# A decoder layer on one core: transposes of the probabilities and of half the gated sum taken from TensorE to VectorE and DMAs, and two FFN pairs computed by seven block products

## The chip, the core and the metric

The kernel runs on one core of one Trainium2 chip. The metric is the device time of one execution in microseconds (us). The engines are TensorE (PE; its weight loads PEld), VectorE (DVE), ScalarE (ACT), GpSimd (POOL) and SyncE (SP). Each takes its own queue of instructions in order, and semaphores let one engine wait for another. DMAs are issued from a queue of SP, ACT or POOL.

## What is computed

One layer of a hybrid decoder for 256 positions, width 1024, FFN width 2816, in float32:

```python
h = rmsnorm(x, norm1_g)
x_rnn, g_rnn, q, k, v, g_br = split(h @ w_in)
ya = rg_lru(causal_dwconv(x_rnn)) * gelu(g_rnn)
yb = attention(rmsnorm(q), rmsnorm(k), v)            # 8 heads of 128, causal
merged = sigmoid(g_A) * (ya @ w_proj_rnn) + sigmoid(g_B) * (yb @ w_proj_attn)
x = x + merged @ w_out
h = rmsnorm(x, norm2_g)
act = gelu(causal_dwconv(h @ w_up)) * (h @ w_gate)
x = x + act @ w_down
```

The sequence fits one block of the sparse attention, so attention is plain and causal. The 2816 FFN columns are 11 blocks of 256.

## The kernel before

**Numbers.** Every product of two float32 matrices is made of three matmuls: each operand is split into a high part (rounded to the format that PE takes) and a low part (the rest), and high·high, high·low and low·high are summed. `mm3` issues the three.

**Weights.** They come in chunks of 1 MB, 128 partitions by 2048. A chunk is loaded by SP into a buffer `raw`, ACT casts it into `hi` (three of them are cast by DVE, `DVE_HI`), DVE writes `lo` = raw - hi, and PE runs 24 matmuls of 128x512 on the two. There are 3 buffers for raw, 4 for hi and 3 for lo; a chunk's lo can be written only when the chunk that held the buffer has been used by PE. In the program before, chunks have numbers (`lo43`); in the one after they are named by their use (`loup0`).

**Stages.** First come the input projections (rx, rg, k, q, v, ga, gb), the recurrence and the attention, then pr and pa (the projections of the two branches), wo (the output projection) and the second norm, then the FFN. In the attention, `att_s` makes a head's scores and its softmax in `sm`, `att_t` transposes the probabilities with three PE transposes and splits them, and `att_o` multiplies them by v. `pa_evac` makes the gated sum `sgb`, and `m_t` transposes a quarter of it with four PE transposes into `mh` and `ml`, which wo reads: blocks 0 and 1 of wo read the first half, blocks 2 and 3 the second. The second norm transposes (`h2T`), multiplies by the norm's weight (`h200` is the first 128 positions, first half of the width; `h210` the second 128 positions) and splits into `h2h` and `h2l`.

**FFN.** Blocks are taken in five pairs and a last one. For pair p, `ffn_half` runs up and gate, each in two halves of the inner dimension (two chunks, 48 matmuls). ACT evacuates the sums into `fs`, and `turn` transposes them: DVE transposes 32x32 squares, four DMAs write to DRAM and one reads back, all issued by SP. Then come the convolution's taps (`fc`), gelu and the product with the gate, which is split into `fah` and `fal`, and `dn` (w_down, accumulated in `acc`) reads them. PE's order is: pair 0, pair 1, pair 2, dn0 dn1, pair 3, dn2 dn3, pair 4, the last block, dn4 to dn9, and the end.

**Order.** Nothing is scheduled by dependences. The program lists every operation and `Later.issue` hands them out in the order of the table `ORDER`, in which "+n" stands for n matmuls; every engine's queue is a part of that one sequence. All instructions therefore bear one line, 296 before and 180 after, and are told apart by their tiles.

Of the kernel before, what the change touches and what calls it, by code (L numbers as in the profile page):

```python
# [7 lines left out]
F32 = mybir.dt.float32  # L8
# [6 lines left out]
P = 128  # L15
# [14 lines left out]
HALVES, SMALLS, WARM, RAWS = 23, 10, 11, 3  # L30
AHEAD_S, AHEAD_L = 2, 3
DVE_HI = (39, 42, 43)
KEPT = {"upd": 2, "gtd": 2, "u": 1, "c": 2, "ah": 3, "al": 3, "s": 1}
UNITS = ("rx0 rx1 rx2 rx3 rg0 rg1 rg2 rg3 k0 k1 k2 k3 ri0 q0 q1 ri1 ga0 ga1 q2 q3 v0 v1 ga2 ga3 v2 v3 gb0 "
         "gb1 gb2 gb3 pr0 pr1 pr2 pr3 pa0 pa1 pa2 pa3")
AFTER = {
    "rx0.0": "s4 stats",
    "rg0.0": "ev0",
    "rg0.3": "ev1",
    "rg1.1": "rx0",  # L40
    "rg1.2": "s5 rx1",
    "rg1.3": "s6 ge0",
    "rg2.1": "xo0",
    "rg3.0": "rgr0",
    "rg3.1": "conv0",
    "rg3.2": "xo1",
    "rg3.3": "s7 ge1",
    "k0.0": "s8 s9",
    "k0.2": "rgr1 conv1",
    "k1.2": "s10 s11",  # L50
    "k1.3": "s12",
    "k2.2": "s13",
    "k2.3": "split0 decay",
    "k3.0": "gelu1 conv2 conv3 split1",
    "k3.3": "s14",
    "ri0.0": "s15",
    "ri0.2": "krs0 ks0",
    "q0.3": "krs1",
    "q1.2": "ks1",
    "q1.3": "s16 rk1",  # L60
    "ri1.3": "rk0",
    "ga0.1": "rq0",
    "ga1.1": "s17 Tk0",
    "q2.0": "s18",
    "q3.0": "s19",
    "q3.2": "Tq0",
    "v0.0": "s20",
    "v1.0": "Tk1",
    "v1.1": "qrs0",
    "v1.2": "S3 s21",  # L70
    "ga2.0": "S2",
    "ga2.1": "rq1 S1 Tq1",
    "ga2.2": "s22 S0 P3",
    "ga2.3": "s23",
    "ga3.0": "s24 s25 la0 la1",
    "ga3.1": "lb1",
    "ga3.2": "lc1 P1 lb0",
# [107 lines left out]
+1 435 +4 444 +1 445 +4 475 +8 446 +2 442 432 +3 391-392 +1 393 +1 464 +3 465 +2 476 +1 478 +8 472 +1 466 474 +1  # L185
# [114 lines left out]
def trunk_layer(ctx: ExitStack, tc: tile.TileContext, xT, x, vec, win_fm, win_tm, wri, wpr, wpa,  # L300
# [23 lines left out]
    class Act:  # L324
# [13 lines left out]
        def pair(self, c):  # L338
            return kt(self.half(c // 2))[:, 2 * (c % 2):2 * (c % 2) + 2, :]


    stream = []

    def add(src):
        stream.append(src)
        return len(stream) - 1

    def two(w, base, c):

        g, kh = c // 2, c % 2  # L350
# [839 lines left out]
```

## Time and profile before

| | before |
|---|---|
| time, median of 3 runs | 434.46 us (434.1 to 435.2) |
| span of the profiled execution; its page gives no other time of its own | 432.3 us |
| granted TensorE clock, mean | 1.000 |
| ACT table loads | 15, 1283 ns each |
| HBM read, written | 89.74 MB, 11.01 MB |
| DMAs of GpSimd's queue | none |

The page gives, for each engine, the time in which it was busy, then 40 slices of the span, and the chain of work that ended last, followed back from the last instruction. Groups of instructions are listed by tile as out<-in with the shape, the count, the busy time and the mean of one in ns, and the idle time ahead of them with what ended it. A timeline row begins with the start and the length in us. Matmuls overlap in PE, so the mean of one (389 ns for 128x512) is not the spacing of two.

### The profile page before, as it was taken

The numbers are of one execution on the slowest core, as the hardware profiler recorded it, in microseconds if no ns is written. First come the engines' busy times: TensorE is split into PE (matmuls) and PEld (weight loads), VectorE is DVE, ScalarE is ACT, GpSimd is POOL, SyncE is SP. The second block draws the span as 40 slices with busy tenths as digits, with TensorE's granted clock in tenths as the row PEclk, the third lists the DMA queues.
The fourth block names the chain that finished last, engine by engine and source line by source line (L and its number), as shares of the span: only waits on it lengthen the run. The fifth ranks groups of instructions, "written<-read, shape, count | busy, mean of one in ns | idle before, by whom it ended". The sixth has DMA issues, their size and how long they took to land.

```text
span 432.3 us, 5409 instructions
## 1 busy us (share of the span) xinstructions
PE 427.6 (99%) x1992; PEld 357.3 (83%) x1992; DVE 324.5 (75%) x417; ACT 271.2 (63%) x307; POOL 51.9 (12%) x101
## 2 busy tenths in 40 slices
PE   9999999999999999999999999999999999999996
PEld 8888888888887888888888888888888888888885
DVE  4867499899898999865666796587888667769633
ACT  5687596886999998853241364468566556456510
POOL 0022483567160000000000000000000000000000
PEclk9999999999999999999999999999999999999999
DMA  7997945999991844474453556898888688788402
GB/s 253 395 394 256 339 169 149 295 314 335 368 313 38 284 142 149 130 238 134 181 194 116 176 203 207 299 325 253 284 265 313 237 270 262 243 286 293 152 0 97
DMA packets 33833, 101.09 MB, mean 234 GB/s; under 512 B 3216, under 2 KB 14096, under 8 KB 30352
## 3 DMA queue, kind: packets, MB, share of 16 engines
q1 hardware_dynamic: 33664, 100.76, 69.1%
q8 instruction: 15, 0.25, 0.2%
q14 instruction: 10, 0.08, 0.0%
q10 hardware_dynamic: 144, 0.00, 0.0%
HBM read 89.74 MB, written 11.01 MB: 233 GB/s over the span
## 4 chain that ended last, share of the span: by engine, by line
PE 87%; DMA 5%; ACT 3%; DVE 2%; issue 2%; SPq 0%; ACTq 0%; DVEq 0%
PE acc L296 14%; PE up L296 13%; PE gt L296 13%; PE rx L296 5%; PE gb L296 5%; PE pr L296 5%; PE yo L296 5%; PE pa L296 5%; PE k L296 5%; PE rg L296 5%; DMA qm<-qd 3%; PE q L296 3%; PE last L296 3%; PE v L296 2%; DMA raw<-in_win_fm 2%
## 5 line engine op out<-in xcount | busy, mean ns | idle before, releaser
L296 DVE TENSOR_TENSOR lo<-raw,hi 128x2048 fp32r<-128x2048 f32 (+1 forms) x72 | 160.3, 2227 | 40.1 <-PE gt L296 10.5
L296 ACT CAST hi<-raw 128x2048 fp32r<-128x2048 f32 (+1 forms) x69 | 128.3, 1862 | 49.7 <-PE gt L296 11.8
L296 PE MATMUL up<-hi,h2h 128*128 128x512 f32 x80 | 31.3, 391 | 0.0
L296 PE MATMUL up<-hi,h2l 128*128 128x512 f32 x80 | 31.2, 389 | 0.0
L296 PE MATMUL up<-lo,h2h 128*128 128x512 f32 x80 | 31.1, 389 | 0.0
L296 PE MATMUL gt<-hi,h2h 128*128 128x512 f32 x80 | 31.1, 389 | 0.0
L296 PE MATMUL gt<-lo,h2h 128*128 128x512 f32 x80 | 31.1, 389 | 0.0
L296 PE MATMUL gt<-hi,h2l 128*128 128x512 f32 x80 | 31.1, 389 | 0.0
L296 PE MATMUL acc<-hi,fah 128*128 128x512 f32 x80 | 31.1, 389 | 0.0
L296 PE MATMUL acc<-lo,fah 128*128 128x512 f32 x80 | 31.1, 389 | 0.0
L296 PE MATMUL acc<-hi,fal 128*128 128x512 f32 x80 | 31.1, 389 | 0.0
L296 POOL TENSOR_TENSOR rsq<-rsq 128x8 f32<-128x8 f32 x32 | 19.2, 600 | 28.6 <-DVE rsq L296 26.3
L296 ACT ACT_TABLE_LOAD x15 | 19.2, 1283 | 1.4 <-PEq L1180 1.2
L296 DVE SCALAR_TENSOR_TENSOR fc<-fu,pv,fc 128x255 f32<-128x255 f32 (+1 forms) x40 | 17.3, 477 | 2.1 <-ACT fc L296 2.1
L296 ACT ACTIVATE fc<-fu,pv 128x256 f32<-128x256 f32 x20 | 10.8, 593 | 11.1 <-DVE fu L296 11.1
L296 PEld LDWEIGHTS up<-hi,h2l 128*128 128x128 f32 x80 | 15.0, 188 | 3.2
L296 PEld LDWEIGHTS acc<-lo,fah 128*128 128x128 f32 x80 | 15.0, 188 | 3.1
L296 PEld LDWEIGHTS acc<-hi,fal 128*128 128x128 f32 x80 | 15.0, 188 | 3.1
L296 PEld LDWEIGHTS gt<-hi,h2l 128*128 128x128 f32 x80 | 15.0, 188 | 3.1
L296 PEld LDWEIGHTS gt<-lo,h2h 128*128 128x128 f32 x80 | 15.0, 188 | 3.1
L296 PEld LDWEIGHTS gt<-hi,h2h 128*128 128x128 f32 x80 | 15.0, 188 | 3.1
L296 PEld LDWEIGHTS acc<-hi,fah 128*128 128x128 f32 x80 | 15.0, 188 | 3.1
(222 smaller groups left out, 1038.8 us busy)
## 6 DMA issues: line engine op xcount, KB each, us to landing
raw<-in_win_fm SPq DMA_DIRECT2D x12, 1024.0 KB, 7.6
raw<-in_win_tm SPq DMA_DIRECT2D x12, 1024.0 KB, 7.2
raw<-in_wdown SPq DMA_DIRECT2D x11, 1024.0 KB, 6.7
raw<-in_wup SPq DMA_DIRECT2D x10, 1024.0 KB, 5.3
raw<-in_wgate SPq DMA_DIRECT2D x10, 1024.0 KB, 7.3
raw<-in_wpr SPq DMA_DIRECT2D x4, 1024.0 KB, 4.8
raw<-in_wpa SPq DMA_DIRECT2D x4, 1024.0 KB, 4.9
raw<-in_wout SPq DMA_DIRECT2D x4, 1024.0 KB, 4.8
```

What stands on the lines that cost most here:

```text
L296: getattr(engine, name)(*map(real, a), **{n: real(v) for n, v in k.items()})
```

## The change

Five things change together, and the table of the order is written anew.

1. **Probabilities.** `att_t` uses `turn`, with 384 columns: a DVE transpose into `pd`, four DMAs to DRAM and one back into `sm`. The two parts of the split are read by `att_o` in the permuted order of columns, runs of 32.
2. **Gated sum.** Its first half is turned in the same way (`md`, `mm`), its second half by PE as before.
3. **FFN pairs 1 and 3.** For a pair, up and gate are one product of two 2x2 block matrices: positions (2 halves) by inner dimension (2 halves), times inner dimension by kind (up, gate). `group` computes it with seven block products in place of eight, from sums and differences of the blocks. `forms` makes four combinations of the normed activations once (R1, S2, S3, S4), and four weight sums are made for each pair: sums 1 and 3 by an accumulating DMA of GpSimd from DRAM into the raw buffer, sums 2 and 4 by DVE. Each product splits its operand (names `b00`, `t1`, `b10`, `b11`, `t2`, `t4`, `t3`) and runs 12 matmuls of 128x512.
4. **Copies.** The copies `fu` ahead of the taps go from DVE to ACT; no weight chunk's hi is cast by DVE any more.
5. **Buffers.** raw has 4 buffers (was 3), `fs` two, PSUM is one pool of eight banks, and the halves are 21 (were 23).

```diff
-HALVES, SMALLS, WARM, RAWS = 23, 10, 11, 3
-DVE_HI = (39, 42, 43)
-KEPT = {"upd": 2, "gtd": 2, "u": 1, "c": 2, "ah": 3, "al": 3, "s": 1}
+HALVES, SMALLS, WARM = 21, 10, 11
+BUFS = {"raw": 4, "hi": 4, "lo": 3}
+SUMS = "dvdv"
+KEPT = {"upd": 2, "gtd": 2, "u": 1, "c": 2, "ah": 3, "al": 3, "s": 2}
...
     def att_t(h):
-        sm = heads[h]
-        ps = bank(f"pt{h}")
-        for b in range(3):
-            nc.tensor.transpose(ps[:, b * P:(b + 1) * P], sm[:, b * P:(b + 1) * P], ident)
-        pth, ptl = small(f"pth{h}", 384, F32R), small(f"ptl{h}", 384, F32R)
-        split2(pth, ptl, ps[:, :3 * P])
+        turn(f"pm{h}", small(f"pd{h}", 384), probs[h], 3, probs[h])
+        a = small(f"ph{h}", 384, F32R), small(f"pl{h}", 384, F32R)
+        split2(*a, probs[h])
+        probs_t[h] = tuple(v.rearrange("p (i u a) -> p u i a", i=4, u=3) for v in a)
...
+        if MT[g]:
+            d = half(f"md{g}")
+            turn(f"mm{g}", d, sgb.half(g))
...
+            for t in range(2):
+                nc.scalar.copy(v(mh)[:, t], d[:, t])
+                nc.vector.tensor_sub(v(ml)[:, t], d[:, t], f(v(mh)[:, t]))
...
+    def forms(name, hi_, lo_, m, new):
...
+        r1, s3, s2, s4 = a11, a10, a00, a01
+        nc.vector.tensor_sub(r1, a11, a10)
+        nc.vector.tensor_sub(s3, a00, a10)
+        nc.vector.scalar_tensor_tensor(s2, r1, -1.0, a00, op0=OP.mult, op1=OP.subtract)
+        nc.vector.scalar_tensor_tensor(s4, a01, -1.0, s2, op0=OP.mult, op1=OP.subtract)
+        for n, v in (("R1", r1), ("S4", s4), ("S2", s2), ("S3", s3)):
+            h, l = new(f"{name}{n}h"), new(f"{name}{n}l")
+            split2(h, l, v)
...
+    def group(name, a, src, rs, nrs, out0, out1, cols=True):
...
+        x = load(f"{name}x", src[0][0])
+        y = load(f"{name}y", src[0][1]) if by["1"] + by["3"] != "dd" else None
+        w, z = load(f"{name}w", src[1][0]), load(f"{name}z", src[1][1])
...
+        product(ps["a"], a["a00"], part("b00", x), True)
+        nc.scalar.activation(o[1][0], ps["a"], AF.Copy, scale=r[0])
+        nc.scalar.activation(o[0][1], ps["a"], AF.Copy, scale=r[1])
+        add("1", x, y, src[0][1])
+        product(ps["c"], a["R1"], part("t1", x), True)
+        nc.scalar.activation(o[1][1], ps["c"], AF.Copy, scale=nrs[:, 1:2])
+        product(ps["a"], a["a01"], part("b10", w), False)
+        nc.scalar.activation(o[0][0], ps["a"], AF.Copy, scale=r[0])
+        product(ps["c"], a["S4"], part("b11", z), False)
+        add("2", x, z, src[1][1])
+        product(ps["b"], a["S2"], part("t2", x), True)
+        nc.vector.scalar_tensor_tensor(o[1][0], ps["b"], r[0], o[1][0], op0=OP.mult, op1=OP.add)
+        nc.vector.scalar_tensor_tensor(o[1][0], ps["c"], nrs[:, 0:1], o[1][0], op0=OP.mult, op1=OP.subtract)
+        add("4", w, x, None)
+        product(ps["d"], a["a11"], part("t4", w), True)
+            add("3", z, None, src[0][1])
+        product(ps["b"], a["S3"], part("t3", y), False)
+        nc.vector.scalar_tensor_tensor(o[0][1], ps["b"], r[1], o[0][1], op0=OP.mult, op1=OP.add)
+        nc.vector.tensor_sub(o[1][1], o[1][1], o[0][1])
+        nc.vector.scalar_tensor_tensor(o[0][1], ps["d"], r[1], o[0][1], op0=OP.mult, op1=OP.add)
...
-            nc.vector.tensor_copy(plain(u, t), d[:, t])
+            FU(plain(u, t), d[:, t])
```

In `add`, "v" is a `tensor_add` of DVE, and "d" a DMA of GpSimd with `accum_op` add, from DRAM. `FU` is ACT's copy. PE's order in the FFN is now: pair 0, the group of pair 1, pair 2, dn0 dn1, the group of pair 3, dn2 dn3, pair 4, and so on as before. `pr3` stands behind `pa1`, so that the second half of pa follows it directly.

**Places in the order.** DVE's queue at the second norm, before:

```order
L296 TENSOR_TENSOR h200_2220<-h2T00_2214,pv_215 128x512
L296 TENSOR_TENSOR h2l0_2233<-h200_2220,h2h0_2226 128x4x128
L296 TENSOR_TENSOR h210_2239<-h2T10_2229,pv_215 128x512
L296 TENSOR_TENSOR xs_181<-yo01_2123,xs_181 128x512
L296 TENSOR_TENSOR h2l0_2233<-h210_2239,h2h0_2226 128x4x128
L296 TENSOR_TENSOR lo43_2255<-raw43_2121,hi43_2195 128x2048
```

and after:

```order
L180 TENSOR_TENSOR h200_2254<-h2T00_2246,pv_133 128x512
L180 TENSOR_TENSOR h210_2272<-h2T10_2264,pv_133 128x512
L180 TENSOR_TENSOR h2l0_2277<-h200_2254,h2h0_2262 128x4x128
L180 TENSOR_TENSOR lof1b00_2283<-rawf1x_2094,hif1b00_2200 128x2048
L180 TENSOR_TENSOR h2l0_2277<-h210_2272,h2h0_2262 128x4x128
L180 TENSOR_TENSOR xs_118<-yo11_2161,xs_118 128x512
```

The long subtraction of a weight chunk, which stood behind the low part of h210, now stands ahead of it.

ACT's queue about the end of pair 0's gate, before (hi48 and hi49 are the two gate chunks of pair 1):

```order
L296 CAST hi48_2398<-raw48_2339 128x2048
L296 ACTIVATE fs0_2391<-up01_2261,rs2_2381 128x512
L296 ACTIVATE fs0_2391<-gt00_2315,rs2_2381 128x512
L296 ACTIVATE fs0_2391<-gt01_2320,rs2_2381 128x512
L296 CAST hi49_2443<-raw49_2373 128x2048
```

and after, where hif1b11 and hif1b10 belong to the group of pair 1:

```order
L180 CAST hif1b11_2445<-rawf1z_2318 128x2048
L180 ACTIVATE fs0_2438<-up01_2290,rs2_2377 128x512
L180 CAST hif1b10_2478<-rawf1w_2366 128x2048
L180 ACTIVATE fs0_2438<-gt00_2348,rs2_2377 128x512
L180 ACTIVATE fs0_2438<-gt01_2356,rs2_2377 128x512
```

A cast now stands ahead of the two evacuations of gate. DVE's queue over the same group, after:

```order
L180 TENSOR_TENSOR lof1t1_2442<-rawf1x_2094,hif1t1_2403 128x2048
L180 TENSOR_TENSOR rawf1x_2094<-rawf1x_2094,rawf1z_2318 128x2048
L180 STREAM_TRANSPOSE fupd0_2468<-fs0_2438 128x8x4x32
L180 TENSOR_TENSOR lof1b11_2476<-rawf1z_2318,hif1b11_2445 128x2048
L180 STREAM_TRANSPOSE fgtd0_2505<-fs0_2438 128x8x4x32
L180 TENSOR_TENSOR lof1b10_2512<-rawf1w_2366,hif1b10_2478 128x2048
L180 TENSOR_TENSOR rawf1w_2366<-rawf1w_2366,rawf1x_2094 128x2048
L180 TENSOR_TENSOR lof1t2_2542<-rawf1x_2094,hif1t2_2521 128x2048
L180 TENSOR_TENSOR lof1t4_2560<-rawf1w_2366,hif1t4_2546 128x2048
L180 TENSOR_TENSOR lof1t3_2582<-rawf1z_2318,hif1t3_2567 128x2048
```

Where four subtractions and two transposes stood for a pair, there are now seven subtractions and two sums about the two transposes, and the transpose of gate stands ahead of lof1b10.

DVE's queue from the middle of the group of pair 3 to dn2 and dn3, after:

```order
L180 TENSOR_TENSOR lof3b10_2900<-rawf3w_2768,hif3b10_2884 128x2048
L180 TENSOR_TENSOR rawf3w_2768<-rawf3w_2768,rawf3x_2601 128x2048
L180 TENSOR_TENSOR lof3t2_2929<-rawf3x_2601,hif3t2_2911 128x2048
L180 TENSOR_TENSOR lof3t4_2943<-rawf3w_2768,hif3t4_2931 128x2048
L180 SCALAR_TENSOR_TENSOR fc1_2863<-fu0_2579,pv_133,fc1_2863 128x255
L180 SCALAR_TENSOR_TENSOR fc1_2863<-fu0_2579,pv_133,fc1_2863 128x254 x4
L180 TENSOR_TENSOR lof3t3_2978<-rawf3z_2723,hif3t3_2951 128x2048
L180 SCALAR_TENSOR_TENSOR fs1_2503<-f3b_2956,rs2_2377,fs1_2503 128x512
L180 TENSOR_TENSOR fc1_2863<-fgtd1_2774,fc1_2863 128x4x128 x2
L180 TENSOR_TENSOR lodn2_3007<-rawdn2_2946,hidn2_2992 128x2048
L180 TENSOR_TENSOR fal1_3021<-fc1_2863,fah1_3010 128x1024
L180 TENSOR_TENSOR lodn3_3027<-rawdn3_2962,hidn3_3016 128x2048
```

All of these stand behind one another from the group's second product on. Before, fal1 stood ahead of the subtraction of pair 3's second chunk, with three more chunks behind it ahead of dn2.

More of the change, by code (lines that the diff above doesn't have):

```diff
@@ new lines @@
+TURN_ACT = ""
+KEPT = {"upd": 2, "gtd": 2, "u": 1, "c": 2, "ah": 3, "al": 3, "s": 2}
+PLAN = """
+rx rg0 rg1 rg2 rg3 decay k0 k1 k2 k3 ri0 q0 q1 ri1 ga0 ga1 q2 q3 v0 v1:3 S3 P3 v1 ga2:1 S2 P2 ga2:1 S1 P1 ga2:1 S0 P0 ga2 ga3 v2:2 S4 P4 v2
+v3:2 S5 P5 v3 O3 gb0:2 O2 gb0 gb1:1 S6 P6 gb1 gb2:1 S7 P7 gb2:1 O1 gb2 O0 gb3:2 O4 gb3 ya0 ya1 pr0 pr1:1 O5 pr1 pr2:2 O6
+pr2 pa0 O7 pa1 pr3 pa2 pa3 wo000 wo010 wo100 wo110 wo001 m2 wo011 wo101 m3 wo111 wo200 wo300 wo210 wo310 wo201 wo301
+n00 wo211 n10 wo311 up00:1 n01 up00:2 n11 up00 gt00 stats2 up01 gt01 G1 up20 up21 gt20 gt21 dn0 dn1 G3 dn2 dn3 up40 up41 gt40 gt41 last0 last1 dn4 dn5 dn6 dn7 dn8 dn9 end
@@ new lines, in trunk_layer, with load @@
+              "up": lambda c: two(wup, 0, c), "gt": lambda c: two(wgate, 0, c),
+              "last": lambda c: [w[NF - 1, :, c * 1024:(c + 1) * 1024] for w in (wup, wgate)],
+              "wo": lambda c: wout[c], "dn": lambda c: wdown[c]}
+    def load(name, src, pieces=1):
+        r = wp.tile([P, 2048], F32, tag="raw", name=f"raw{name}", bufs=BUFS["raw"])
+        if isinstance(src, list):
+            n = 2048 // len(src)
+            for a, v in enumerate(src):
+                nc.sync.dma_start(r[:, a * n:(a + 1) * n], v)
+        elif len(src.shape) == 3:
+            nc.sync.dma_start(r.rearrange("p (c n) -> p c n", c=2), src)
+        else:
+            n = src.shape[-1] // pieces
+            for a in range(pieces):
+                nc.sync.dma_start(r[:, a * n:(a + 1) * n], src[:, a * n:(a + 1) * n])
+        return r
@@ new lines, in split @@
+    def split(name, r, n=2048, on_dve=False, m=1):
+        h = wp.tile([P, 2048], F32R, tag="hi", name=f"hi{name}", bufs=BUFS["hi"])
+        l = wp.tile([P, 2048], F32R, tag="lo", name=f"lo{name}", bufs=BUFS["lo"])
+        if name in LO_DMA:
+            nc.scalar.copy(h[:, :n], r[:, :n])
+            nc.scalar.activation(l[:, :n], r[:, :n], AF.Copy, scale=-1.0)
+            nc.gpsimd.dma_start(l[:, :n], r[:, :n], accum_op=OP.add)
+            return h, l
+        for a in range(m):
+            s = slice(a * n // m, (a + 1) * n // m)
+            (nc.vector.tensor_copy if on_dve else nc.scalar.copy)(h[:, s], r[:, s])
+            nc.vector.tensor_sub(l[:, s], r[:, s], f(h[:, s]))
+        return h, l
@@ L419, in split2, with chunk @@
+    def chunk(kind, c, n=2048, **k):
+        return split(f"{kind}{c}", load(f"{kind}{c}", source[kind](c)), n, **k)
     def split2(dh, dl, src):
@@ L631, in rx_evac @@
         turned_x[g] = half(f"xd{g}")
-        turn(f"xm{g}", turned_x[g], scaled(half(f"xs{g}"), rx_ps[g], rs1), f"rx{g}")
+        turn(f"xm{g}", turned_x[g], scaled(half(f"xs{g}"), rx_ps[g], rs1))
     def rx_order(g):
@@ new lines, in rx_all @@
+    def rx_all():
+        for g in range(2):
+            rx_ps[g] = [bank(f"rx{g}{t}") for t in range(2)]
+        for a in range(KT // 2):
+            for g in range(2):
+                for cs in (slice(0, 1), slice(1, 2)) if (a, g) == (0, 0) else (slice(0, 2),):
+                    for kk in range(2):
+                        k = 2 * a + kk
+                        h, l = shi[a, g][:, cs, kk], slo[a, g][:, cs, kk]
+                        for n, (x, w) in enumerate(((xgh, h), (xgl, h), (xgh, l))):
+                            for t in range(2):
+                                nc.tensor.matmul(rx_ps[g][t].rearrange("p (c n) -> p c n", c=2)[:, cs],
+                                                 x[k][:, t * P:(t + 1) * P], w, start=k == n == cs.start == 0,
+                                                 stop=k == KT - 1 and n == 2, skip_group_check=True)
+        norm1_stats()
+        for g in range(2):
+            rx_evac(g)
+            rx_order(g)
+            for c in (2 * g, 2 * g + 1):
+                rx_conv(c)
+            ri_split(g)
@@ new lines, in unit @@
+    def unit(kind, c):
+        if kind == "ri":
+            w = chunk(kind, c, 1024)
+            for n4 in range(4):
+                ri(c, w, n4)
+                if n4 == 3:
+                    lru(c)
+                yield
+            return
+        w = chunk(kind, c)
+        g, kh = c // 2, c % 2
+        if not kh:
+            open_ps[kind] = [bank(f"{kind}{g}{t}") for t in range(2)]
+        ps = open_ps[kind]
+        for k4 in range(4):
+            tm_mm(ps, w, 4 * kh + k4, k4, *{"pr": (yah, yal), "pa": (ybh, ybl)}.get(kind, (xgh, xgl)),
+                  kind not in "qkv")
+            if kh and k4 == 3:
+                evac[kind](g, ps)
+            yield
@@ new lines, in x_forms, with rg_group @@
+    def x_forms():
+        m = {}
+        for t in range(2):
+            for kh in range(2):
+                v = m[t, kh] = small(f"xf{t}{kh}", 512)
+                nc.vector.tensor_mul(v.rearrange("p (k t) -> p k t", t=P), kt(xTs.half(kh))[:, :, t * P:(t + 1) * P],
+                                     g1[:, 4 * kh:4 * kh + 4, None].to_broadcast([P, 4, P]))
+        return forms("xf", xgh, xgl, m, lambda n: small(n, 512, F32R))
+    xf = []
+    def rg_group():
+        if not xf:
+            xf.extend((x_forms(), negative(rs1, "nrs1")))
+        s = [half(f"gs{g}") for g in range(2)]
+        src = [[source["rg"](2 * g + kh) for g in range(2)] for kh in range(2)]
+        yield from group("rg", xf[0], src, rs1, xf[1], *s)
+        for g in range(2):
+            rg_turn(g, s[g])
@@ L999, in norm2_stats @@
         rsqrt(ss2[:, 0, :], rs2, 1.0 / D, 2)
+        xf[:] = [forms("hf", h2h, h2l, h2, lambda n: small(n, 512, F32R)), negative(rs2, "nrs2")]
     acc, act, kept = {}, {}, {}
@@ L1018, in trunk_layer, with ffn_out, pair_act @@
     turned, gated = {}, {}
-    def pair_up(p):
+    FU = nc.scalar.copy
+    def ffn_out(kind, p, s):
+        d = half("fld") if kind == "last" else keep(kind + "d", p)
+        turn(f"{kind}m{p}", d, s)
+        v = d.rearrange("p (i t c b) -> p t c i b", i=4, t=2, c=4)
+        turned["last" if kind == "last" else (kind, p)] = v
+        if kind == "last":
+            last_block()
+        elif ("up", p) in turned and ("gt", p) in turned:
+            pair_act(p)
+    def pair_act(p):
         d = turned["up", p]
@@ L1125, in trunk_layer @@
+    NP = NF // 2
+    for token in PLAN.split():
+        step(token)
     with tc.manual_schedule():
```

606 lines of the change are left out of this document (199 added, 407 removed), and 82 rows, old and new, of the table ORDER.

## The prediction

> **What bounds the kernel now.** I read the page's busy shares and its slices first, then the chain that ended last, then what TensorE (PE) waited for, to see whether any other engine is ever late.
>
> ```profile
> span 432.3 us, 5409 instructions
> PE 427.6 (99%) x1992; PEld 357.3 (83%) x1992; DVE 324.5 (75%) x417; ACT 271.2 (63%) x307; POOL 51.9 (12%) x101
> PE   9999999999999999999999999999999999999996
> DVE  4867499899898999865666796587888667769633
> PEclk9999999999999999999999999999999999999999
> PE 87%; DMA 5%; ACT 3%; DVE 2%; issue 2%; SPq 0%; ACTq 0%; DVEq 0%
> PE warm L296 <- DVE ones L296: 1.0, 1, 1.0
> PE pt L296 <- DVE sm L296: 0.4, 1, 0.4
> 271.19 10.88 PE up L296 x48
> 282.07 10.88 PE gt L296 x48
> ```
>
> PE is busy in every slice but the last, and inside the program it waits once, 0.4 us. The two last rows are steps of the chain (start, length): 48 matmuls of 128x512 in 10.88 us, so **226.7 ns each, back to back**. The span is the sum of PE's work, so a matmul taken away is worth its whole time, and any lateness that the change brings to DVE, ACT or a DMA costs its whole time too. I use this spacing, not the mean of one instruction, which counts overlap twice. The span is 432.3 us and the median of the runs 434.46: 2.16 us lie outside the span, and I add them at the end.
>
> **What leaves PE.**
>
> ```profile
> 139.16 0.70 PE pt L296 x3
> 148.09 0.70 PE s L296 x6
> 151.52 0.33 PE pt L296 x3
> 141.93 0.64 PE o L296 x6
> 225.67 0.44 PE mT L296 x4
> ```
>
> Pairs 1 and 3 of the FFN had 96 matmuls each and have seven products of 12, 84: 24 fewer, 24 x 0.2267 = 5.44 us. The probabilities' transposes were 8 groups of 3 at 0.33, 2.64 us, and the first took 0.70, which holds PE's only wait: 0.37 more. Of four mT groups two go to the stream transpose: 2 x 0.44 = 0.88. Together **9.33 us**. Against it, the o matmuls now read the probabilities in runs of 32 elements. The s group, whose operands are already read in such runs, takes 0.70 where o takes 0.64: 0.06 x 8 = 0.5 us, with ends 0 and 0.5. PE's own work falls by **8.8 us**.
>
> **What DVE and ACT get.** The rows with their means, and a stretch of DVE's timeline for the spacing:
>
> ```profile
> L296 DVE TENSOR_TENSOR lo<-raw,hi 128x2048 fp32r<-128x2048 f32 (+1 forms) x72 | 160.3, 2227 | 40.1 <-PE gt L296 10.5 <-issue 9.1 <-PE rg L296 7.0
> L296 ACT CAST hi<-raw 128x2048 fp32r<-128x2048 f32 (+1 forms) x69 | 128.3, 1862 | 49.7 <-PE gt L296 11.8 <-PE pr L296 6.5 <-PE pa L296 5.7
> L296 DVE STREAM_TRANSPOSE fupd<-fs 128x1024 f32<-128x1024 f32 x5 | 6.2, 1241 | 0.5 <-ACT fs L296 0.5
> L296 DVE COPY fu<-fupd 128x512 f32<-128x512 f32 x10 | 3.8, 418 | 5.6 <-DMA fupd<-upm 5.6
> L296 DVE CAST hi<-raw 128x2048 fp32r<-128x2048 f32 x3 | 3.7, 1218 | 0.0
> ...
> 245.91 0.68 DVE L296 TENSOR_TENSOR h<-h2T,pv 128x512 f32<-128x512 f32 x1
> 246.51 0.68 DVE L296 TENSOR_TENSOR xs<-yo,xs 128x512 f32<-128x512 f32 x1
> 247.28 0.69 DVE L296 TENSOR_TENSOR h2l<-h,h2h 128x512 fp32r<-128x512 f32 x1
> 247.89 2.29 DVE L296 TENSOR_TENSOR lo<-raw,hi 128x2048 fp32r<-128x2048 f32 x1
> 250.10 0.68 DVE L296 TENSOR_TENSOR xs<-yo,xs 128x512 f32<-128x512 f32 x1
> ...
> 289.53 0.87 DVE L296 SCALAR_TENSOR_TENSOR fc<-fu,pv,fc 128x255 f32<-128x255 f32 x2
> ```
>
> One lo subtraction occupies DVE 2.2 us (247.89 to 250.10), a 512-wide operation 0.6 (245.91 to 246.51). A group splits seven 2048-wide operands where the pair split four: 6 more lo subtractions in all, and 4 weight sums of the same width, which I price alike: 22 us. The forms and the groups' evacuations add some 18 operations of 512, 10.8 us; eight transposes of 384 and one of 1024 add 8 x 0.5 + 1.2 = 5.2 (0.5 is the row of 1024, scaled). The fu copies (3.8) and three hi casts (3.7) leave. DVE gains about 30 us, to 355 of some 428, 83%. ACT gets nine hi casts of 1.86 and 16 copies and casts of 512, priced at DVE's 0.6: 26 us. On average both fit beside PE; so the price is local, at the places where DVE's queue is now the longer one. I followed each place as a chain, from the rows above.
>
> **Second norm.**
>
> ```profile
> 243.89 1.39 PE yo L296 x6
> 245.27 0.44 PE h2T L296 x4
> ```
>
> Call the end of h2T10 T. PE still has one wo group (1.36) and five matmuls of up00 before the sixth, which takes h210's low part: 1.36 + 5 x 0.227 = 2.49. DVE now does mul (0.6), h200's low part (0.6), lof1b00 (2.2), and only then h210's low part (0.6), 4.05 with the start: **1.6 us late**. Before, the low part came ahead of the long subtraction. Ends 0.9 (mul starts early) and 1.6.
>
> **Group of pair 1, third product.** ACT casts hif1b10 before it evacuates gt.
>
> ```profile
> 270.55 1.43 ACT L296 ACTIVATE fs<-gt,rs 128x512 f32<-128x512 f32 x2 [2.21 <-PE gt L296]
> 271.87 1.91 ACT L296 CAST hi<-raw 128x2048 fp32r<-128x2048 f32 x1
> ```
>
> From the end of gt01: cast 1.9 (it waits for gt's hi buffer), two evacuations 1.4, DVE's transpose 1.2, then lof1b10 2.2: 6.7 us. PE has two products, 24 x 0.2267 = 5.44, and one matmul that needs no low part, 0.23. **1.1 us late.** If DVE comes late out of the forms, up to 2.2. From there it does 2.2 us of subtraction for each product of 2.72, plus one sum; it stays just ahead.
>
> **dn2 behind the group of pair 3.** From the end of the group's first product DVE has lof3b10, a sum, t2, t4, t3 (11.0), five tap operations (two take 0.87, so 2.2), one evacuation and two products with the gate (1.8), lodn2 (2.2) and fal1 (1.2): 18.4 us, against 6 x 2.72 + 0.45 = 16.8 on PE. 1.6 us late with an empty queue at the start, 2.3 if dn2's load, issued some 9 us ahead, lands late too. I take **1.8**.
>
> **wo behind the turned half of the gated sum.** A turn goes over DRAM; its issues on SP and the landing of its read-back:
>
> ```profile
> 274.47 3.00 SPq L296 DMA_DIRECT2D gtm<-fgtd  x4
> 283.16 0.33 SPq L296 DMA_DIRECT2D fgtd<-gtm  x1
> fgtd<-gtm SPq DMA_DIRECT2D x5, 512.0 KB, 4.2
> ```
>
> The read-back goes out 8.7 us after the first write and lands 4.2 later, 12.9 in all. From pa1's end: four 512-wide operations 2.6, transpose 1.2, the turn 12.9, one copy to mh 0.6: 17.3 us. PE has pr3, pa2 and pa3, 72 x 0.2267 = 16.3. That is 1.0 late; DMA there is busy half the time (0.9 in the stretch of the rows), so it may be earlier. Ends 0 and 1.9, the latter if wo3's load ahead of the read delays it. I take **0.7**.
>
> Sum: 432.3 - 8.8 + 1.6 + 1.1 + 1.8 + 0.7 = 428.7, and with 2.16 **430.9 us**.
>
> **What I cost at nothing, and its cover.**
>
> ```profile
> raw<-in_wup SPq DMA_DIRECT2D x10, 1024.0 KB, 5.3
> raw<-in_wgate SPq DMA_DIRECT2D x10, 1024.0 KB, 7.3
> raw<-in_wdown SPq DMA_DIRECT2D x11, 1024.0 KB, 6.7
> 140.00:160.00 20.00, 20.00 (x100) 16.81 (x99) 18.68 (x34) 19.49 (x24) 0.00 (x0) 1.00 0.63 209
> 160.00:180.00 20.00, 20.00 (x106) 16.98 (x105) 18.56 (x31) 17.25 (x23) 0.00 (x0) 1.00 0.48 158
> ```
>
> *The probabilities' way over DRAM*: 12.9 us by the turn above, of 384 columns where that has 1024; 18 to 22 us of PE work lie between each transpose and its o. The reads wait on SP with weight loads queued behind, but the fourth raw buffer lets loads go about 14 us ahead there. Without that cover a head costs a few us.
>
> *The accumulating loads*: four loads of 1 MB become DMAs of the idle GpSimd queue that add to a buffer. The trace has none. Below, a plain load, 5.3 us; above, two loads of 7.3, since it reads the destination as well, 14.6. I take 9, nearest the plain wgate load with some for the read. rawf1z is issued after lof1b11 and read by hif1t3 about 10 us later, so 9 is hidden and what exceeds 10 is not. rawf1x has 11 to 13 us, rawf3x more.
>
> The Trainium skill (DMA: Bandwidth & Descriptors, Anatomy of one DMA, SWDGE path) fits a GpSimd DMA by 2.0 us plus bytes over 436e3, for 1 MB an estimate of 4.4 us; by it the sum stays as it is. No run here shows such a DMA, and that page's fit is for a plain one.
>
> *DVE in attention* is 18.6 of 20 us busy and gets 4 us of transposes between 130 and 200 us, where four hi and three lo buffers cover it; the price without cover is under rival three.
>
> **Rivals.**
>
> *One, slower: the accumulating loads land late.* With landing time L both groups wait L - 10 us ahead of their last products. At 14.6 that is 2 x 4.6 = 9.2, so 440.1. It cancels the gain at 2 x (L - 10) = 3.6, L = 11.8. For it: two streams in one DMA, beside a DMA share of 0.8 to 0.9 in the FFN of before. Against it: 11.8 is 1.6 times the slowest plain load. 15%, 435 to 440.
>
> ```profile
> 5.75 0.77 PE L296 MATMUL rx<-his,xgh 128*128 128x256 f32 x2
> 7.44 0.40 PE L296 MATMUL rx<-his,xgl 128*128 128x256 f32 x2
> ```
>
> These pairs of equal matmuls show PE at half speed until about 7 us from the start. A long wait could bring that state back: 12 matmuls at twice 0.227 are 2.7 us on top, per group, so 445.5 at worst. The Trainium skill (TensorE: Matmul & The Clock Gate, Part 1) has the gate close after an idle window of about 3.4 us; the pace at the start agrees, but the profile's PEclk line reads full there, and no wait here is long enough to test it. I give this 3 of the 15%.
>
> *Two: none of the four places is late.* If DVE reaches them with its queue empty and the buffers come free early, only PE's work counts: 434.46 - 8.8 = 425.7. For it: DVE idles 40.1 us ahead of lo rows. Against it: all four chains are fixed by the order. 12%.
>
> *Three: DVE's queue is full more widely*, in attention (up to 4 us) or about the groups, where 5 evacuations and two transposes, 5.4 us each, stand ahead of the next chunks' lo. It decides once DVE's slack of 1.4 us in 20 is used up. 430.9 + 2 to 4.4 = 432.9 to 435.3. 18%.
>
> **How the numbers follow.** The forecast, 430.9 within 428 to 432.6, has 55%, rival one 15, two 12, three 18. 8 in 10 needs both neighbours and the lower part of rival one: 425.6 to 436.2. A measurement of this kernel tells about 0.3%, 1.3 us, from no change. Faster by more than that is below 433.2: the forecast, rival two and a little of rival three, 0.70. Within: the rest of three and the start of one, 0.17. Slower, above 435.8: 0.13, nearly all of it rival one.
>
> **What would show it.** PE's rows: 84 matmuls a group, no pt, 8 mT, and waits on DVE at the second norm, before the third product of pair 1 and at dn2, 1 to 2 us each, and at wo for the turned half. The accumulating loads' time to landing against 10 us. o groups at 0.64 or 0.70. It would be wrong if PE waits in attention, if a group waits on hif1t3 or hif3t3, or if lo subtractions take longer than 2.2 us.

## The result and the profile after

The changed kernel takes **440.66 us** (439.41 to 442.19, 4 runs) where the kernel before takes 434.39 (434.1 to 435.2, 4 runs): a ratio of 1.0143, 95% interval 1.0118 to 1.0167. It is slower, by 1.4%. The prediction was 430.9, within 425.6 to 436.2, with 0.70 for faster; it was wrong in sign and in range.

The page of the changed kernel, the rows that answer to those shown of before:

```profile
span 438.6 us, 5440 instructions
PE 424.1 (97%) x1936; PEld 351.6 (80%) x1936; DVE 353.0 (80%) x439; ACT 295.6 (67%) x332; POOL 54.5 (12%) x105
PE   8999999999979999999999899999999799999996
DVE  3776699689698999954875599979989699798733
PEclk9999999999999999999999999999999899999999
PE 79%; DMA 8%; DVE 6%; issue 3%; ACT 3%; SPq 0%; DVEq 0%; POOLq 0%; ACTq 0%
```

Totals came out as forecast: DVE 353.0 us busy (forecast 355), ACT 295.6 (297). What differs are three slices between the first and the last in which PE is not full (7, 8 and 7 tenths) and a chain that runs more through DMA and DVE (8% and 6%, where it was 5% and 2%). PE's rows in the view of waits (us in total, times, longest) name the places; two at the program's start are left out:

```profile
PE s L180 <- DVE mx L180: 3.2, 1, 3.2
PE f3b L180 <- DVE fs L180: 2.8, 1, 2.8
PE up L180 <- DVE h2l L180: 1.3, 1, 1.3
PE f1b L180 <- DVE fs L180: 1.0, 1, 1.0
PE f1a L180 <- DVE lof1b L180: 0.9, 1, 0.9
PE acc L180 <- DVE fal L180: 0.4, 1, 0.4
```

Three of the six were forecast: the second norm (`up` on `h2l`), the group of pair 1 (`f1a` on `lof1b`) and dn2 (`acc` on `fal`). The two longest and `f1b` were not.

The span can be cut at matmuls that both kernels have. Each number is the difference of two such starts in the timeline; the last three columns belong to experiments told below. Each column is one profiled execution; that of s1_after is the fastest of its ten (433.98 us, where the median is 435.47).

| stretch, us | before | after | s1_after | both | plain_pairs |
|---|---|---|---|---|---|
| start to first rg | 28.60 | 29.36 | 28.91 | 29.03 | 29.04 |
| rg to first wo (attention) | 195.55 | 196.35 | 191.44 | 191.61 | 191.44 |
| first wo to gt00 (second norm) | 30.55 | 31.97 | 31.96 | 31.99 | 29.99 |
| gt00 to up of pair 2 (pair 1) | 38.09 | 38.12 | 38.34 | 36.95 | 38.08 |
| up of pair 2 to dn0 | 21.76 | 21.76 | 21.78 | 21.80 | 21.76 |
| dn0 to up of pair 4 (pair 3, dn2) | 43.51 | 46.49 | 45.14 | 42.65 | 43.52 |
| up of pair 4 to the end | 74.24 | 74.55 | 74.53 | 74.57 | 74.37 |
| span | 432.30 | 438.60 | 432.10 | 428.60 | 428.20 |

**Attention.** It should have become some 3 us shorter and became 0.8 longer. The timeline of PE (start, length, what; in brackets the idle time and what ended it), at the scores of one head:

```profile
126.81 0.28 PE L180 MATMUL s<-kTl,qTh 128*128 128x256 f32 x1
130.26 0.58 PE L180 MATMUL s<-kTh,qTl 128*128 128x256 f32 x1 [3.17 <-DVE mx L180]
130.64 0.63 PE L180 MATMUL ga<-higa,xgh 128*128 128x512 f32 x1
131.06 0.63 PE L180 MATMUL ga<-loga,xgh 128*128 128x512 f32 x1
```

and DVE's, at the same time:

```profile
126.03 2.29 DVE L180 TENSOR_TENSOR lov<-rawv,hiv 128x2048 fp32r<-128x2048 f32 x1
128.31 0.40 DVE L180 CUSTOM_DVE_ANT_0 sm<-s,mask 128x256 f32<-128x256 f32 x1
...
129.93 0.25 DVE L180 CUSTOM_DVE_ANT_0 sm<-s,mask 128x128 f32<-128x128 f32 x1
130.12 0.08 DVE L180 DVE_READ_ACCUMULATOR2_ANT mx<- 128x1 f32 x1
```

Six matmuls make a head's scores, three for its first 128 positions and three for the second, all into one tile `s`. PE stops ahead of the sixth. In between lies DVE's reduction of the first half (`sm` with `mx`, 128x128 at 129.93), which reads the same tile; it stands behind a `lov` subtraction of 2.29 us and the softmax of another head. The new table puts that reduction between the fifth and the sixth matmul of this head, and PE's sixth carries a wait for DVE, as the order says:

```
571 L180 MATMUL s_1274<-kTl_985,qTh_1037 128x256
572 L180 MATMUL s_1274<-kTh_927,qTl_1049 128x256 [waits DVE_49]
```

In the table of before every such reduction stands behind its own head's sixth matmul. The `ga` matmuls after the wait start 0.42 us apart, not 0.227: PE runs at half clock, as the windows view says (length, busy time and count of each engine, granted clock, DMA share, GB/s):

```profile
130.20:132.00 1.80, 1.74 (x5) 1.46 (x6) 1.09 (x5) 1.61 (x6) 0.38 (x2) 0.50 0.97 298
349.00:351.50 2.50, 2.50 (x7) 1.94 (x7) 1.59 (x2) 2.50 (x3) 0.00 (x0) 0.50 0.97 392
```

The second row is the other long wait, in the group of **pair 3**. Its accumulating load `rawf3z` and what follows it, over POOL, ACT, DVE and PE:

```profile
331.25 1.20 POOL L180 DMA_DIRECT2D rawf3z<-in_wgate  x1 [25.38 <-DMA rawlast<-in_wgate]
343.00 1.91 ACT L180 CAST hif3t<-rawf3z 128x2048 fp32r<-128x2048 f32 x1 [4.66 <-DMA rawf3z<-in_wgate]
344.95 2.29 DVE L180 TENSOR_TENSOR lof3t<-rawf3z,hif3t 128x2048 fp32r<-128x2048 f32 x1 [2.76 <-ACT hif3t L180]
347.16 0.74 DVE L180 SCALAR_TENSOR_TENSOR fs<-f3b,rs,fs 128x512 f32<-128x512 f32 x1
348.05 0.47 PE L180 MATMUL f3b<-hif3t,hfS3h 128*128 128x512 f32 x1 [2.79 <-DVE fs L180]
```

Issued at 331.25, landed 11.7 us later; then cast, subtraction, and an evacuation of the bank `f3b` which the last product writes again, and only then PE. That evacuation reads what an earlier product left in the bank, complete soon after `f3d` began at 342.34, and DVE stood idle for 2.76 us ahead of the subtraction: it is in this chain only because the order puts it behind. No run moves it. The chain of pair 1 has the same form (start, length, what):

```profile
277.72 10.09 DMA rawf1z<-in_wgate
...
287.89 1.92 ACT hif1t L180
...
292.05 0.75 DVE fs L180
292.94 3.03 PE f1b L180 x12
```

### The profile page after: what moved, and what is told of

It reads as the page before. It is cut to its first block, busy times and chain, and to the rows that moved or that the text cites. A ratio compares the mean times of both kernels' runs of the same rounds, so it can differ in the third digit from the quotient of the medians.

```text
span 438.6 us, 5440 instructions
## 1 busy us (share of the span) xinstructions
PE 424.1 (97%) x1936; PEld 351.6 (80%) x1936; DVE 353.0 (80%) x439; ACT 295.6 (67%) x332; POOL 54.5 (12%) x105
## 4 chain that ended last, share of the span: by engine, by line
PE 79%; DMA 8%; DVE 6%; issue 3%; ACT 3%; SPq 0%; DVEq 0%; POOLq 0%; ACTq 0%
PE acc L180 13%; PE up L180 7%; PE gt L180 7%; PE gb L180 5%; PE pr L180 5%; PE pa L180 5%; PE k L180 5%; PE rg L180 5%; PE yo L180 5%; PE ga L180 5%; PE rx L180 4%; PE q L180 4%; DMA rawf3z<-in_wgate 3%; PE v L180 2%; PE last L180 2%
## 5 line engine op out<-in xcount | busy, mean ns | idle before, releaser
L180 PE MATMUL acc<-hidn,fal 128*128 128x512 f32 x80 | 31.2, 390 | 0.4 <-DVE fal L180 0.4
L180 PE MATMUL acc<-hidn,fah 128*128 128x512 f32 x80 | 31.1, 389 | 0.0
L180 PE MATMUL acc<-lodn,fah 128*128 128x512 f32 x80 | 31.1, 389 | 0.0
L180 DVE TENSOR_TENSOR lodn<-rawdn,hidn 128x2048 fp32r<-128x2048 f32 x11 | 25.1, 2285 | 1.7 <-ACT hidn L180 0.9
L180 ACT CAST hidn<-rawdn 128x2048 fp32r<-128x2048 f32 x11 | 20.9, 1903 | 0.6 <-PE acc L180 0.5
L180 PE MATMUL up<-hiup,h2l 128*128 128x512 f32 x48 | 18.8, 392 | 1.3 <-DVE h2l L180 1.3
L180 PE MATMUL up<-hiup,h2h 128*128 128x512 f32 x48 | 19.0, 395 | 0.0
L180 PE MATMUL up<-loup,h2h 128*128 128x512 f32 x48 | 18.7, 389 | 0.0
L180 PE MATMUL gt<-higt,h2h 128*128 128x512 f32 x48 | 18.7, 389 | 0.0
L180 PE MATMUL gt<-logt,h2h 128*128 128x512 f32 x48 | 18.7, 389 | 0.0
L180 ACT CAST higt<-rawgt 128x2048 fp32r<-128x2048 f32 x6 | 11.5, 1915 | 10.1 <-PE acc L180 3.5
```

The lines of the kernel that those rows point to most:

```text
L180: getattr(engine, name)(*map(real, a), **{n: real(v) for n, v in k.items()})
```

## The experiments

Every kernel was timed beside the kernel before on its chip, which took 434.3 to 434.9 there. In the diffs of the order, the table is written out by names.

**s1_after: the reduction moved.**

```diff
 PE  s1 <- kTl0,qTh0   (fifth matmul)
-DVE sm1,mx1 <- s1,mask 128x128
 PE  s1 <- kTh0,qTl0   (sixth matmul)
+DVE sm1,mx1 <- s1,mask 128x128
```

> Only the place of one instruction changes: VectorE's reduction of the first half of head 1's scores comes behind the sixth matmul of these scores, not ahead of it. Theory A (this place makes PE wait 3.2 us, and the half clock behind it costs 1.2 us more): about 4.3 us less than the changed kernel, 436.4 us; PE's wait on mx is gone and the granted clock between 130 and 134 us is 1.0. Rival B (VectorE is simply full there, and the wait comes back at a later matmul of the attention): less than 1.5 us gained, 439 us or more.

435.47 us (433.98 to 436.81, 10 runs), ratio 1.0024 [1.0008, 1.0039]: 5.2 us less than the changed kernel, for one instruction moved past one in the common sequence. No engine's own queue changes by it; what goes is PE's wait for DVE ahead of the sixth matmul. The wait on `mx` is gone, the stretch of attention is 191.44 us in place of 196.35, and the clock is full there. So the wait of 3.2 us and the half clock behind it were the loss in attention. What is left of the two unforeseen waits in the groups, in the fastest execution:

```profile
PE f3b L180 <- DVE fs L180: 1.4, 1, 1.4
PE f1b L180 <- DVE fs L180: 1.2, 1, 1.2
```

In seven of the ten executions the mean granted clock was 0.995 or 0.996, not 1.000 as in this one. So in most of them the clock fell somewhere, and the waits of the median execution may be longer than these; no trace shows one.

**no_sum3: the changed kernel without the two late accumulating loads.** It leaves out the third weight sum of pairs 1 and 3, so that the last product of each group multiplies the plain chunk and the result is not the layer's; only its time is used.

```diff
-            add("3", z, None, src[0][1])
+            pass
```

> Leaves out the third weight sum of both groups, the two accumulating loads into rawf1z and rawf3z; all the rest is the changed kernel. Theory A (the late landing of these loads makes PE wait ahead of t3): the waits of 1.1 and 2.9 us ahead of t3 go, with the half clock behind the second one, 1.7: 5 to 6 us less, about 435 us. Rival B (VectorE's queue is late there anyway, and its evacuation that PE waits for comes no earlier): less than 2 us gained, 438.7 or more.

434.93 us (432.49 to 437.56, 10 runs), ratio 1.0015 [0.9993, 1.0036]: 5.7 us less than the changed kernel. The waits of `f1b` and `f3b` are gone, and those of `s` (3.9 in this profile), `up`, `f1a` and `acc` have stayed. Two waits of 1.0 and 2.8 and ten matmuls at 0.2 us too much are 5.8 together. The run takes away the traffic of two loads as well as their lateness; that the lateness was the loss rests on the two chains above.

**both: the two together**, to see whether these are two losses or one. Like no_sum3 it leaves out the third weight sum.

> This is the kernel with the reduction of s1's first half behind PE's sixth matmul, and without the two accumulating loads of sum 3 (the third weight sum of pairs 1 and 3 is left out, so the last product of each group uses the plain chunk). Theory A, the late reduction in attention and the late accumulating loads are two separate losses: they add, 440.66 - 5.2 - 5.7 = 429.8 us, and PE's waits that are left are those at the second norm (up on h2l, 1.3), before the third product of pair 1 (0.9) and at dn2 (0.6 to 1.5). Theory B, they share a cover: where attention runs 4.9 us earlier the groups' own waits on f1b and f3b were already 1.0 to 1.4 us shorter, so taking the loads away brings only those waits, 435.47 - 1.2 - 1.4 = 432.9 us.

430.39 us (429.96 to 430.69, 5 runs), ratio 0.9901 [0.9885, 0.9918]. They add: 10.3 us less than the changed kernel, where 5.2 and 5.7 make 10.9. The waits that are left are three of those forecast:

```profile
PE up L180 <- DVE h2l L180: 1.3, 1, 1.3
PE warm L180 <- DVE ones L180: 1.1, 1, 1.1
PE f1a L180 <- DVE lof1b L180: 0.9, 1, 0.9
PE acc L180 <- DVE fal L180: 0.6, 1, 0.6
```

(The wait of `warm` is that of the program's start, 1.0 before.) The time lies 0.5 us from the prediction.

**dma_price: what an accumulating load takes by itself.** Five transfers of the same 1 MB are put into the quiet end of s1_after, each waiting for the one before.

```diff
+    def probe():
+        src = pairs(wgate, 0, 0)
+        r = load("probe", src)
+        v = r.rearrange("p (c n) -> p c n", c=2)
+        nc.gpsimd.dma_start(v, src)
+        nc.gpsimd.dma_start(v, src, accum_op=OP.add)
+        nc.gpsimd.dma_start(v, src, accum_op=OP.add)
+        nc.sync.dma_start(v, src)
```

> The run s1_after with five transfers of 1 MB added in the quiet stretch at the end, one after the other into one buffer that nobody reads: a plain load by SP, a plain one by GpSimd's queue, two accumulating ones by GpSimd, and a plain one by SP. They may run past the end of the rest, so its time is not compared. Theory A (an accumulating load has a price of its own, about two loads): 8 to 10 us each against 4 to 5 of a plain one, alone as well as beside other traffic. Rival B (its 8.4 to 11.7 us come from the traffic beside it): about the plain load's time, 5 us.

GpSimd's queue (the idle time in brackets is the wait for the transfer before), then SP's:

```profile
410.29 0.75 POOL L180 DMA_DIRECT2D rawprobe<-in_wgate  x1 [83.03 <-DMA rawprobe<-in_wgate]
417.68 1.20 POOL L180 DMA_DIRECT2D rawprobe<-in_wgate  x1 [6.64 <-DMA rawprobe<-in_wgate]
426.32 1.20 POOL L180 DMA_DIRECT2D rawprobe<-in_wgate  x1 [7.44 <-DMA rawprobe<-in_wgate]
434.67 0.38 SPq L180 DMA_DIRECT2D rawprobe<-in_wgate  x1
```

From issue to the next issue the plain load of GpSimd takes 7.4 us and the two accumulating ones 8.6 and 8.4. From issue to landing GpSimd's three took 8.3 in the median and SP's two 6.0, so an accumulating load takes 1.4 times a plain one of SP. Beside the other loads of the FFN it took 8.5 to 11.7 in the changed kernel, and 12.4 once in the kernel both. So an accumulating load has a price of its own, smaller than the two loads of theory A, and only some 1.1 us above GpSimd's own plain load; what is above 8.6 came only beside other traffic. The time of this kernel is not compared, as it does more.

**fill_g3: is the half clock a price of its own?** Twelve unused matmuls fill PE's wait in the group of pair 3.

```diff
+        if name == "f3":
+            for _ in range(12):
+                nc.tensor.matmul(ps["a"], a["S4"][0][:, 0, :], a["S4"][0].rearrange("p k t -> p (k t)"), start=True, stop=True,
+                                 skip_group_check=True)
         product(ps["b"], a["S3"], part("t3", y), False)
```

> Adds 12 matmuls of 128x512, whose result is not used, to PE's wait ahead of t3 in the group of pair 3. Theory A (an idle time of nearly 3 us brings PE to half clock, and that costs 1.7 us): the ten slow matmuls of t3 run at 0.23 us, 1.5 to 1.7 us less than the changed kernel, about 439 us, though PE has 2.7 us more work. Rival B (these matmuls are slow for another reason, as their operands or the DMAs beside them): no gain, or up to 0.5 us more.

PE's timeline there, the filling and two matmuls of the product behind it:

```profile
344.99 2.89 PE L180 MATMUL f3a<-hfS4h 128*128 128x512 f32 x12
...
348.44 0.39 PE L180 MATMUL f3b<-hif3t,hfS3h 128*128 128x512 f32 x1
348.67 0.39 PE L180 MATMUL f3b<-lof3t,hfS3h 128*128 128x512 f32 x1
```

The product now runs at full pace in this execution, as it should if the half clock came from the wait. The time, 440.33 us (438.77 to 442.28, 4 runs), ratio 1.0133 [1.01, 1.0166], is the same: dn2 behind it waits 0.9 us for `lodn` and 0.6 for `fal`, where it had waited 0.4. In this one place the half clock was hidden behind the next late operand. That the wait slows the product came out as expected, the gain did not.

**act_order: who makes dn2 late.** In s1_after, ACT casts a chunk of the last block ahead of dn2's own operand; here it stands behind.

```diff
 ACT hif3t3 <- rawf3z
-ACT hilast0 <- rawlast0
 ACT fc <- fc, fu <- fupd, hidn2 <- rawdn2, fah1 <- fc
+ACT hilast0 <- rawlast0
```

> The run s1_after with the hi cast of last0 on ACT moved from ahead of dn2's chain (gelu, hidn2, fah1) to behind fah1. Theory A (dn2 waits because a 1.9 us cast that nobody needs yet stands ahead of hidn2): PE's waits on lodn2 and fal1 (0.9 and 0.6) shrink to 0.6 or less together, about 1 us less than s1_after, 434.5. Rival B (VectorE, and not ACT, is what is late there): no change, 435.5.

434.79 us (433.6 to 435.93, 10 runs), ratio 1.001 [0.9992, 1.0027]: 0.7 less than s1_after, but the intervals overlap, so a gain is not shown. DVE's `lodn` starts 1.9 us after the evacuation of `f3b` in place of 2.9, so the cast did make it late. The waits of `acc` are gone, but not by that alone: in the profiled run `f3b` waited 2.0 us (its load took 10.9), PE then ran at half clock for 3 us, and so came to dn2 1.4 us later after the product's start than in s1_after:

```profile
343.00:346.00 3.00, 3.00 (x9) 2.32 (x8) 3.00 (x2) 2.98 (x3) 0.00 (x0) 0.50 0.78 320
```

**norm_swap: the old order at the second norm.**

```diff
-DVE lof1b00 <- rawf1x,hif1b00
 DVE h2l0 <- h210,h2h0
+DVE lof1b00 <- rawf1x,hif1b00
```

> Only the long subtraction lof1b00 at the second norm comes behind the low part of h210. Theory A (the order on VectorE is the cause of the wait): PE's wait of 1.3 us on h2l goes, 1.4 to 1.9 us less than the changed kernel, about 439 us. Rival B (the 2.2 us are only put off, since VectorE is full up to the group of pair 1, and the accumulating load into rawf1x starts later): PE waits as much in the group, less than 0.5 us gained.

441.68 us (439.87 to 442.95, 4 runs), ratio 1.0159 [1.0125, 1.0193], no gain. The wait at the norm is gone, and others have come or grown in the group of pair 1 (the profiled execution is the slowest of the four):

```profile
PE f1b L180 <- DVE fs L180: 1.8, 1, 1.8
PE f1a L180 <- ACT fs L180: 1.2, 1, 1.2
```

The windows view of the changed kernel has DVE (third pair of numbers) busy for 19.56 of 20 us from there on:

```profile
260.00:280.00 20.00, 19.92 (x88) 16.09 (x86) 19.56 (x24) 12.45 (x15) 1.21 (x1) 1.00 0.56 192
```

ACT's evacuation, for which `f1a` waits, had itself waited 1.5 us for DVE's transpose `fgtd`. With so little slack, 2.2 us of subtraction moved back come out at the next place.

**pool_sums: the two DVE sums of each pair given to GpSimd**, in s1_after.

```diff
-                nc.vector.tensor_add(to, to, tile_)
+                nc.gpsimd.tensor_add(to, to, tile_)
```

> The run s1_after with weight sums 2 and 4 of both groups made by GpSimd and not by VectorE. Theory A (VectorE is full in the groups, and that delays the reads ahead of the accumulating loads): rawf1z's load starts 1 to 2 us earlier, PE's wait ahead of t3 of pair 1 (1.2) goes, 434 us. Rival B (a sum of 128x2048 takes GpSimd much longer than VectorE's 2.3 us, or slows VectorE beside it): PE waits for t2 and t4, 437 us or more.

439.69 us (439.43 to 439.84, 4 runs), ratio 1.0128 [1.0107, 1.0149]: 4.2 us more than s1_after. Two of GpSimd's sums and the subtractions of DVE that fell beside them:

```profile
266.42 4.62 POOL L180 TENSOR_TENSOR rawf1x<-rawf1x,rawf1z 128x2048 f32<-128x2048 f32 x1 [17.97 <-DVE lof1t L180]
268.77 4.42 DVE L180 TENSOR_TENSOR lof1b<-rawf1z,hif1b 128x2048 fp32r<-128x2048 f32 x1 [1.34 <-PE gt L180]
276.66 4.63 POOL L180 TENSOR_TENSOR rawf1w<-rawf1w,rawf1x 128x2048 f32<-128x2048 f32 x1 [1.63 <-DVE lof1b L180]
276.88 6.55 DVE L180 TENSOR_TENSOR lof1t<-rawf1x,hif1t 128x2048 fp32r<-128x2048 f32 x1 [0.37 <-ACT hif1t L180]
```

A sum takes 4.6 us there (6.6 once) where DVE takes 2.29. Both subtractions started while a sum ran, and each ended 2.1 us after the sum did (273.19 after 271.04, 283.43 after 281.29), which is nearly the whole 2.29 of a subtraction that runs alone: in these two rows DVE got on only when GpSimd had done. The groups wait for the operands at `f3d` (1.8) and `f3a` (1.2).

**both_start: the table load at the start.** The changed table issues ACT's first load of an activation table late, and ACT meets its first one at 4.5 us, behind the landing of x. The kernel both, with that load moved to the front:

```diff
 ACT g1 <- in_vec, SP xT0 <- in_xT, DVE ones, SP raws0 <- in_win_fm
+ACT preload of the table
 PE  warm <- ones
```

> As the kernel before in this call, with ScalarE's table load moved from late in the order back to the start, behind the issue of the first small load. Theory A, that load (1.28 us at 4.47 in the changed kernel, behind the landing of x) delays the first activations and with them every matmul: the first rg group starts at 28.8 in place of 29.5 and the time is 0.4 to 0.8 us lower. Theory B, the start is set by the landing of the first weights: rg stays at 29.1 to 29.5 and the time within 0.3 us.

430.73 us (430.23 to 431.06, 5 runs), ratio 0.9908 [0.9891, 0.9924]. The first rg starts 0.3 us earlier, then waits 0.3 for its weights' low part, and nothing of it is left at wo. What makes the start of the changed kernels 0.3 to 0.8 us longer stays open.

**plain_pairs: the parts that pay.** The probabilities, the turned half of the gated sum and four raw buffers are kept, with the reduction behind the sixth matmul; from wo on the order of before, pairs 1 and 3 as plain pairs, no forms and no sums, `fu` copies on DVE again.

```diff
-... up00 gt00 stats2 up01 gt01 G1 up20 up21 gt20 gt21 dn0 dn1 G3 dn2 dn3 ...
+... up00 gt00 stats2 up01 gt01 up10 up11 gt10 gt11 up20 up21 gt20 gt21 dn0 dn1 up30 up31 gt30 gt31 dn2 dn3 ...
-    FU = nc.scalar.copy
+    FU = nc.vector.tensor_copy
+        if f"{kind}{c}" in ("up0", "gt0"):
+            k["on_dve"] = True
```

> The changed kernel up to wo with head 1's reduction behind its matmuls, and from wo on the order of before: pairs 1 and 3 plain with 96 matmuls each, no sums, no combinations, fu copies and two hi casts on VectorE. So it keeps parts 1 and 2 of the change alone (probabilities and half the gated sum). Theory A (the block products give back more than they save: 5.4 us saved, and 1.9 at the second norm, 3.0 in the group of pair 1 and 4.3 in that of pair 3 lost): 3 to 5 us less than the run s1_after, 430 to 432 us, below the kernel before. Rival B (the block products are worth their 5.4 us, and the losses are of the new order from wo on and its buffers): 436 us or more.

**429.98 us** (429.95 to 430.18, 4 runs), ratio 0.9906 [0.9882, 0.9931]: faster than the kernel before, by 0.9%, and than the changed one, and it computes all of the layer. Its waits:

```profile
PE warm L178 <- DVE ones L178: 1.1, 1, 1.1
PE rx L178 <- ACT his L178: 0.2, 1, 0.2
```

## Why the prediction was wrong

**DVE in attention: the step that failed first.** The prediction priced it at nothing, since 4 us of transposes would be covered by four hi and three lo buffers, and let rival three hold the price of a full queue. That was an average of one engine. The loss was one instruction: a reduction set between two matmuls of the scores tile that it reads, so that PE waited for DVE's queue, 3.2 us and the clock after it, 4.9 in the stretch. The buffers of hi and lo had no part in it: s1_after has the same ones. It would have been seen if each head's reductions had been compared, in the order of after, with the matmuls of their own tile.

**The accumulating loads: the budget was short and the load long.** "rawf1z is issued after lof1b11 and read by hif1t3 about 10 us later, so 9 is hidden and what exceeds 10 is not." The landing times were 10.1 and 11.7 and PE waited 1.0 and 2.8: the budget was 9.1 (10.1 - 1.0) and 8.9 (11.7 - 2.8), not 10. The cast is not what PE waits for; behind the landing come 1.9 of cast, 2.2 of subtraction and 0.7 of an evacuation. My value of 9 would just have been hidden; the two landed 1.1 and 2.7 above it. The mechanism was rival one, at 15%; its threshold, 11.8, stood too high twice over: with a budget of 9 the same sum gives 10.8, and the half clock, which I kept for the worst case, came at 11.7 already.

**What held.** With both causes away the time is 430.39, and the stretches of that kernel show the terms. PE waits 1.3 us at the second norm (forecast 1.6), 0.9 ahead of the third product (1.1); dn2's `acc` waits 0.6, while the whole stretch of pair 3 and dn2 is 42.65, where 43.51 less 12 matmuls of 0.2267 plus the forecast 1.8 give 42.6. That agreement is in part luck. By the starts of the matmuls (322.26, 341.88 and 354.03), dn2 and dn3 took 12.15 where 48 matmuls of 0.2267 are 10.88, so 1.3 late and not 1.8; and the seven products took 19.62 where 84 of 0.2267 are 19.04, a loss of 0.6 that no term held. In attention the stretch falls by 4.1 by s1_after. The terms that leave in it (2.64, 0.37 and one mT group of 0.44) less 0.5 are 3.0; the o groups took 0.64 as before, so the 0.5 was not due, and some 0.7 of the gain stay unexplained. The wait of wo for the turned half (0.7) did not come. That the total of this kernel lies so near is luck as well: attention came 1.7 shorter than the terms had it, with the 0.7 of wo, and what lies outside the span 0.4 shorter, while the start took 0.4, the second norm 0.3, pair 1 0.5 and the end 0.3 longer.

**The five parts are not one change.** Against plain_pairs, the kernel both has 24 matmuls less, 5.44 us, and is no faster. By the table it gives back 2.0 us at the second norm; in pair 1 it gains 1.1 of 2.72 and in pair 3 0.9 of 2.72. 5.44 less 2.0, 1.6 and 1.8 is nothing. Of these 5.4 about 1.0 is the pace of the groups, whose matmuls start every 0.232 to 0.234 us and not every 0.227; the rest comes with the waits for DVE at the second norm, in pair 1 and at dn2. The gain of plain_pairs comes with the probabilities, the gated sum and the fourth raw buffer, which no run tries apart; the seven products, even with sum 3 left out, pay for their saved matmuls mostly with DVE's time.

## What to carry to other kernels

Where an order is written out by hand, check for each operation that reads a matmul's tile whether another matmul into that tile still follows it; such a place costs the whole lateness of the reader's queue, however idle that engine is on average. The budget of a transfer ends at the matmul that waits, not at the first reader: take off each step in between. On an engine without slack, moving a late operation back only names a new place of waiting, so take the parts of a change apart before judging it.

## What the runs showed of the hardware

**Half clock after short waits.** In the profiled executions the granted clock fell to 0.50, mostly for about 3 us, in or behind PE waits of 3.9, 3.4, 3.2, 2.8, 2.7, 2.6, 2.0 and 1.8 us. The Trainium skill (TensorE: Matmul & The Clock Gate, Part 1) has the clock fall after an idle window of about 3.4 us, which is longer than the last six of these waits. It also calls the count of slow matmuls run-variable because the window runs freely, and that agrees: of the ten executions of no_sum3 one has a mean granted clock of 1.000, the others 0.990 to 0.996. Nor does the length of one wait decide it in these runs. In norm_swap the clock stayed full for 6 us after a wait of 2.3 us, and then fell behind two of 0.9 and 0.6, as PE's starts show, first 0.22 us and then 0.42 apart:

```profile
354.34 0.50 PE L180 MATMUL acc<-hidn,fal 128*128 128x512 f32 x1 [0.63 <-DVE fal L180]
354.68 0.39 PE L180 MATMUL acc<-hidn,fah 128*128 128x512 f32 x1
354.90 0.39 PE L180 MATMUL acc<-lodn,fah 128*128 128x512 f32 x1
...
356.32 0.63 PE L180 MATMUL acc<-hidn,fal 128*128 128x512 f32 x1
356.74 0.63 PE L180 MATMUL acc<-hidn,fah 128*128 128x512 f32 x1
```

In fill_g3 the same two waits left it full. A forecast should take half clock as possible from 1.8 us on, and behind shorter waits that stand close together.

**An accumulating load** takes 8.4 to 8.6 us for 1 MB from one issue to the next, with no other load beside it (dma_price), and GpSimd's plain load 7.4. The fit of the Trainium skill (DMA: Bandwidth & Descriptors, Anatomy of one DMA), by which the prediction set an estimate of 4.4 beside its sum, lies well below the plain one here.

**DVE beside GpSimd.** In the rows of pool_sums a subtraction of DVE that started during a sum of GpSimd, both on 128x2048 in float32, took 4.42 and 6.55 us, and ended 2.1 us after the sum; alone it takes 2.29.
